# Rope angles traced one step later, and the row swaps of q and k issued by SyncE a step after their products

## The chip, the cores and the metric

The kernel runs on one core of a Trainium2 chip. The metric is the device time of one execution in microseconds (us). PE is TensorE, ACT ScalarE, DVE VectorE, POOL GpSimd, and SP SyncE, which only issues DMAs here.

## The reference

Two decoder layers on a (1, 1024, 1024) float32 stream. Each layer projects the stream with one wide matrix, runs three token mixers on the result, merges them with gates, projects back and normalises; then a gated MLP with a short convolution. The change touches the partial rotary embedding of q and k in the attention mixer, the first quarter (16) of each head's 64 channels:

```python
def rope_tables(positions):
    inv_freq = ROPE_THETA ** (-jnp.arange(0, ROT_DIM, 2, dtype=jnp.float32) / ROT_DIM)
    ang = positions.astype(jnp.float32)[..., None] * inv_freq
    return jnp.cos(ang), jnp.sin(ang)

def apply_partial_rope(t, cos, sin):
    half = ROT_DIM // 2
    x1, x2, rest = tf[..., :half], tf[..., half:ROT_DIM], tf[..., ROT_DIM:]
    out = jnp.concatenate([x1 * c - x2 * s, x2 * c + x1 * s, rest], axis=-1)
...
    proj = jnp.einsum('bsd,de->bse', x, w_in)
    u_pool, q, k, v, xc, gate_b, gate_c, gate_logits = jnp.split(proj, ...)
    q = apply_partial_rope(q.reshape(B, S, N_Q_HEADS, HEAD_DIM), cos, sin)
    k = apply_partial_rope(k.reshape(B, S, N_KV_HEADS, HEAD_DIM), cos, sin)
```

## The kernel before

Channels lie on the 128 partitions and the 1024 positions along the free axis. Every float32 operand is split into a high part (`scalar.copy` to fp32r, line 90) and a remainder (a subtraction, line 94, on DVE or POOL), and each product is three matmuls (lines 110 to 112).

The input projection of a layer works through 20 **pairs** of 128-column weight tiles, by a Strassen-like scheme of seven block products. One block product (`run`) is four blocks of three matmuls, 12 matmuls of 128x512. A pair has two halves. `begin` loads the first weight tile (`load(0)`, 512 KB, line 707, issued by SP), splits its two blocks and makes two runs (B11, B21); ACT copies the first sum out of PSUM (line 727). `rest` loads the second weight tile (`load(1)`, also line 707), forms block sums on POOL (line 741, then line 738 three times: a21, a11, and last a12), splits the results (`made`), and makes five runs in the order T2, T1, T3, T4, B22. The first of these, T2, needs the operand `w2`, which is `made(a11)`: it exists only after `load(1)` has landed, POOL has run lines 741, 738 and 738, and ACT has cast it. T2 also overwrites the PSUM bank that line 727 copies. Lines 759, 762 and 764 (DVE) put the pair's two outputs `ca` and `cb` together; 764 comes last and completes `ca`. Then `then(ca, cb)` hands them on.

`run_pairs` sets the order: begin, rest, begin, rest; the first two and the last two pairs are interleaved differently. After each half `due()` advances a tick and calls what `after(ticks, f)` has set aside, so `after(2, f)` called inside the `rest` of one pair runs f after the `begin` of the next pair and before its `rest`. Counting from 0, pair 2 makes k and v, pairs 4 and 6 make two 128-channel chunks of q each, and the pairs between make gates. The same holds in both layers.

For k and for each chunk of q, `turn` calls `swapped`: ACT copies the chunk (line 340), then four DMAs of 8 rows (32 KB each, lines 342 and 343) overwrite 32 rows of the copy with the partner rows. `rotate` (DVE, lines 349 to 351) follows by `after(3)`, and the split and the stores to DRAM by `after(4)`.

The cosine and sine tables: `rope_tables` (lines 156 to 178) fetches the positions by eight small POOL DMAs, works out angles on DVE (lines 163 to 170) and ACT (171 to 174), and ACT writes rows to DRAM. `rope_spread` (lines 182 to 193) has SP copy these rows over the partitions. At the start of layer 0, `second()` (lines 230 to 252) forms the blocks T2, T1, T3, T4 and B22 of the input on DVE and ACT.

The program is traced under

```python
with self.tc.manual_schedule(engines={mybir.EngineType.SP, mybir.EngineType.PE}):
```

SP and PE therefore issue in the order of the program text. The order on ACT, DVE and POOL is chosen by a planner when the program is built: from what it estimates to be ready, with the earlier place in the program as the priority.

Buffers that matter here: three weight tiles (`ws`), six split operands (`w`), three tiles `pt` (swap copies, and the sine table).

Of the kernel before, what the change touches and what calls it, by code (L numbers as in the profile page):

```python
# [60 lines left out]
class Trunk:  # L61
# [274 lines left out]
    def swapped(self, c):  # L336

        nc = self.nc
        swp = self.new([P, S], F32, "pt")
        nc.scalar.copy(swp[:], c[:])  # L340
        for base in (0, 64):
            nc.scalar.dma_start(swp[base:base + 8, :], c[base + 8:base + 16, :])
            nc.scalar.dma_start(swp[base + 8:base + 16, :], c[base:base + 8, :])
        return swp

    def rotate(self, c, swp, cos, sin):
# [28 lines left out]
    def project(self, l, first):  # L375

        nc = self.nc
        st = {}

        def turn(c, put):  # L380
            swp = self.swapped(c)
            self.after(3, lambda: self.rotate(c, swp, *self.tab))
            self.after(4, lambda: put(*self.parts(swp, c)))

        def kv(k, v):
            if l:
                self.load_tables()

            def put(hi, lo):
                for n in range(2):  # L390
                    own, other = slice(64 * n, 64 * n + 64), slice(64 - 64 * n, P - 64 * n)
                    self.store(self.kd[n, own], hi[own])
                    self.store(self.kd[n, other], lo[own])

            def keys_first():
                for c in range(2):
                    pt = self.bank()
                    for i in range(4):
                        b = 4 * c + i
                        nc.tensor.transpose(pt[:, i * P:(i + 1) * P], v[:, b * P:(b + 1) * P], self.ident[:])  # L400
                    t = self.new([P, 2, HALF], F32, "pt")
                    t = t[:].bitcast(F32R)
                    self.split(t[:, 0], t[:, 1], pt[:])
                    self.store(self.vd[:, :, c * HALF:(c + 1) * HALF].rearrange("a p c -> p a c"), t)

            turn(k, put)
            self.after(2, keys_first)

        def qq(i):
            def then(*c):  # L410
                for j in range(2):
                    def put(*x, j=j):
                        for n in range(2):
                            self.store(self.qd[:, :, n, 2 * i + j, :].rearrange("b c q -> c b q"),
                                       x[n].rearrange("c (b q) -> c b q", q=P))
                    turn(c[j], put)
            return then
# [48 lines left out]
        made, second = first or (None, None)  # L466
        if second:
            self.pend.append(lambda: None)
            self.pend.append(lambda: (second(), self.rope_tables()))
            self.after(4, self.parameters)  # L470
            self.after(2, self.rope_spread)
        self.run_pairs([self.pair([self.ins["w_in"][l, 2 * n + i] for i in range(2)], True, then,
# [628 lines left out]
```

## Time and profile before

| | |
|---|---|
| time, three runs | 2769.86, 2775.11, 2777.68 us; median 2775.11 |
| profiled execution, own time | 2775.4 us |
| its span | 2773.4 us |
| mean granted PE clock | 0.971 |
| busy: PE, DVE, POOL, ACT | 93%, 69%, 53%, 44% of the span |
| SP and ACT DMA issues | SP issues all weight loads; ACT the gates and 40 row swaps |

The profiled execution is one run taken by the hardware profiler; its span is the time from its first to its last instruction, and 2.0 us of its own time lie around that. In a timeline each row has the start and the duration in us, the engine (a trailing q: the engine's sequencer, as for a DMA issue), the line, the operation, the tiles (out<-in), how many instructions were merged (x), and in brackets the idle time before it and what ended that. PE busy is not PE at its peak, because matmuls are pipelined.

### The profile page before, as it was taken

How to read it: one execution, taken by the hardware profiler on the slowest of the kernel's cores; microseconds unless marked ns; L12 is line 12 of the kernel's file. 1: busy time of each engine (PE TensorE's matmuls, PEld its weight loads, DVE VectorE, ACT ScalarE, POOL GpSimd, SP SyncE). 2: the span in 40 equal slices, each digit the busy share in tenths (PEclk: the TensorE clock that was granted, in tenths of full speed). 3: DMA queues.
4: the chain of work that ended last, by engine and by line, in shares of the span. 5: the costliest groups of instructions: out<-in, count | busy, mean ns of one | idle time of the engine just before them, and what ended most of it. 6: DMA issues, size and time to landing. Idle time of an engine off the chain costs nothing.

```text
span 2773.4 us, 32010 instructions
## 1 busy us (share of the span) xinstructions
PE 2583.8 (93%) x11408; PEld 2105.9 (76%) x11408; DVE 1919.5 (69%) x2310; ACT 1233.4 (44%) x2050; POOL 1457.2 (53%) x962
## 2 busy tenths in 40 slices
PE   5989999998899999899889999999988999998887
PEld 4868887787688888677667788777867888877676
DVE  6565556737887877786675656477478887767866
ACT  4434445523544554434444444454335455544343
POOL 2554456767466555370434545566674556553701
PEclk8999999999999999999899999999999999999999
DMA  3433358554133333674323423765532333327742
GB/s 123 138 114 107 108 196 225 161 181 150 57 104 114 114 99 107 222 277 134 106 95 117 142 75 108 237 189 164 201 122 75 96 107 103 114 92 266 267 139 76
DMA packets 163232, 389.59 MB, mean 140 GB/s; under 512 B 17408, under 2 KB 48896, under 8 KB 162048
## 3 DMA queue, kind: packets, MB, share of 16 engines
q1 hardware_dynamic: 136496, 293.02, 32.3%
q0 software_dynamic: 14848, 55.09, 7.0%
q10 hardware_dynamic: 11728, 39.45, 3.7%
q8 instruction: 89, 1.46, 0.2%
q14 instruction: 71, 0.58, 0.1%
HBM read 281.75 MB, written 104.43 MB: 139 GB/s over the span
## 4 chain that ended last, share of the span: by engine, by line
PE 49%; DVE 16%; issue 5%; DMA 3%; ACT 3%; POOL 3%; ACTq 0%; DVEq 0%; SPq 0%; POOLq 0%
PE b L111 16%; PE b L112 16%; PE b L110 16%; DVE w L94 3%; DVE X L94 2%; DVE st L259 1%; DVE ve L275 1%; DMA X<-in_w_down 1%; POOL ws L738 1%; DVE pt L811 1%; ACT w L90 1%; POOL w L94 1%; DVE t L290 1%; DMA X<-h_blocks 1%; DVE w L321 0%
## 5 line engine op out<-in xcount | busy, mean ns | idle before, releaser
L110 PE MATMUL b<-X,w 128*128 128x512 f32 x2552 | 1014.1, 397 | 55.1 <-ACT s L727 20.0
L112 PE MATMUL b<-X,w 128*128 128x512 f32 x2552 | 1008.3, 395 | 27.9 <-DVE w L94 18.6
L111 PE MATMUL b<-X,w 128*128 128x512 f32 x2552 | 1006.5, 394 | 3.2 <-DVE X L94 3.2
L94 DVE TENSOR_TENSOR w<-ws,w 128x512 fp32r<-128x512 f32 (+1 forms) x454 | 450.4, 996 | 358.5 <-ACT w L90 346.3
L90 ACT CAST w<-ws 128x512 fp32r<-128x512 f32 (+1 forms) x608 | 408.0, 677 | 489.6 <-PE b L112 154.5
L110 PEld LDWEIGHTS b<-X,w 128*128 128x128 f32 x2552 | 487.4, 191 | 167.5 <-ACT s L727 24.6
L112 PEld LDWEIGHTS b<-X,w 128*128 128x128 f32 x2552 | 486.9, 191 | 136.4 <-DVE w L94 22.5
L94 POOL TENSOR_TENSOR w<-ws,w 128x512 fp32r<-128x512 f32 (+2 forms) x154 | 297.5, 1934 | 532.5 <-ACT w L90 520.3
L111 PEld LDWEIGHTS b<-X,w 128*128 128x128 f32 x2552 | 487.3, 191 | 105.9 <-DVE X L94 5.5
L741 POOL TENSOR_TENSOR ql<-ws 128x512 f32<-128x512 f32 x82 | 125.0, 1524 | 354.8 <-DMA ws<-in_w_in 254.0
L111 PE MATMUL b<-w,w 128*128 128x512 f32 x528 | 214.4, 406 | 48.5 <-DVE w L94 41.3
L110 PE MATMUL b<-w 128*128 128x512 f32 x528 | 211.1, 400 | 2.7 <-DVE pt L905 1.4
L112 PE MATMUL b<-w,w 128*128 128x512 f32 x528 | 210.6, 399 | 0.0
L111 PEld LDWEIGHTS b<-w,w 128*128 128x128 f32 x528 | 102.0, 193 | 82.4 <-DVE w L94 54.3
L738 POOL TENSOR_TENSOR ws<-ws,ws 128x512 f32<-128x512 f32 x82 | 142.4, 1736 | 6.2
L811 DVE SCALAR_TENSOR_TENSOR q<-t,par,q 128x1023 f32<-128x1023 f32 x88 | 127.4, 1448 | 19.0 <-ACT q L808 18.1
L94 DVE TENSOR_TENSOR w<-X,w 128x512 fp32r<-128x512 f32 (+1 forms) x107 | 121.5, 1158 | 22.3 <-ACT w L90 22.3
L738 POOL TENSOR_TENSOR ws<-ql,ws 128x512 f32<-128x512 f32 x82 | 125.0, 1524 | 6.3
L738 POOL TENSOR_TENSOR ws<-ws 128x512 f32<-128x512 f32 x82 | 118.6, 1446 | 16.9 <-DVE w L94 12.7
L110 PEld LDWEIGHTS b<-w 128*128 128x128 f32 x528 | 102.0, 193 | 28.3 <-DVE t L905 2.7
L811 DVE SCALAR_TENSOR_TENSOR pt<-t,par,pt 128x1023 f32<-128x1023 f32 x88 | 123.3, 1401 | 0.2
L112 PEld LDWEIGHTS b<-w,w 128*128 128x128 f32 x528 | 102.1, 193 | 20.6
(242 smaller groups left out, 3783.6 us busy)
## 6 DMA issues: line engine op xcount, KB each, us to landing
ws<-in_w_up SPq DMA_DIRECT2D x88, 512.0 KB
ws<-in_w_in SPq DMA_DIRECT2D x75, 512.0 KB
gates<-t ACTq DMA_DIRECT2D x48, 512.0 KB
ws<-in_w_o SPq DMA_DIRECT2D x40, 512.0 KB
h_blocks<-t SPq DMA_DIRECT2D x80, 256.0 KB
s<-h_blocks SPq DMA_DIRECT2D x66, 256.0 KB
t<-gates SPq DMA_DIRECT2D x32, 512.0 KB
t<-q_parts POOLq DMA_DIRECT2D x64, 256.0 KB, 4.1
```

The lines of the kernel that those rows point to most:

```text
L90: self.nc.scalar.copy(hi, src)
L94: return eng.tensor_tensor(lo, src, hi.bitcast(F32), op=ALU.subtract)
L110: self.nc.tensor.matmul(out, wh, xh, start=start and i == 0, stop=False, skip_group_check=more)
L111: self.nc.tensor.matmul(out, wh, xl, start=False, stop=False, skip_group_check=more)
L112: self.nc.tensor.matmul(out, wl, xh, start=False, stop=stop and i == n - 1, skip_group_check=more)
L259: self.nc.vector.bn_stats(st[:, c, :], z[:, c * HALF:(c + 1) * HALF])
L275: nc.vector.scalar_tensor_tensor(ve[:], ve[:], r[:], r[:], op0=ALU.mult, op1=ALU.mult)
L290: nc.vector.scalar_tensor_tensor(z[:], z[:], mv[:, 0:1], g[:], op0=ALU.subtract, op1=ALU.mult)
L738: sub = lambda out, x, y: nc.gpsimd.tensor_tensor(out, x, y, op=ALU.subtract)
L741: nc.gpsimd.tensor_tensor(s1[:], a21, a22, op=ALU.add)
L811: nc.vector.scalar_tensor_tensor(y[:, d:], c[:, :S - d], w(k), y[:, d:], op0=ALU.mult, op1=ALU.add)
```

## The change

Three edits. `swapped` issues its four DMAs on SP (`nc.sync`) and no longer on ACT. `turn` calls `swapped` two ticks later: after the `begin` of the next pair, ahead of its `rest`; `rotate` and the split stay at ticks 3 and 4. `rope_tables` is called one tick on, after the `rest` of the first pair, and not right behind `second()`.

```diff
@@ swapped
         for base in (0, 64):
-            nc.scalar.dma_start(swp[base:base + 8, :], c[base + 8:base + 16, :])
-            nc.scalar.dma_start(swp[base + 8:base + 16, :], c[base:base + 8, :])
+            nc.sync.dma_start(swp[base:base + 8, :], c[base + 8:base + 16, :])
+            nc.sync.dma_start(swp[base + 8:base + 16, :], c[base:base + 8, :])
@@ project
         def turn(c, put):
-            swp = self.swapped(c)
-            self.after(3, lambda: self.rotate(c, swp, *self.tab))
-            self.after(4, lambda: put(*self.parts(swp, c)))
+            swp = []
+            self.after(2, lambda: swp.append(self.swapped(c)))
+            self.after(3, lambda: self.rotate(c, swp[0], *self.tab))
+            self.after(4, lambda: put(*self.parts(swp[0], c)))
...
         if second:
             self.pend.append(lambda: None)
-            self.pend.append(lambda: (second(), self.rope_tables()))
+            self.pend.append(second)
+            self.after(1, self.rope_tables)
             self.after(4, self.parameters)
             self.after(2, self.rope_spread)
```

## The prediction

> **What bounds the kernel now.** I read the page first, then the waits of PE in the two input projections, then the timelines of the engines around each swap.
>
> ```profile
> span 2773.4 us, 32010 instructions
> PE 2583.8 (93%) x11408; PEld 2105.9 (76%) x11408; DVE 1919.5 (69%) x2310; ACT 1233.4 (44%) x2050; POOL 1457.2 (53%) x962
> ```
>
> PE sets the pace, so any time that PE stands still in a projection goes onto the end. Its waits, first for 0 to 400 us (layer 0), then for 1400 to 1850 us (layer 1), as total, times, longest:
>
> ```profile
> PE b L110 <- ACT w L90: 15.2, 1, 15.2
> PE b L110 <- ACT s L727: 9.1, 5, 4.4
> ...
> PE b L110 <- ACT s L727: 8.9, 4, 4.8
> ```
>
> One wait of 15.2 us at the start (it ends at 36.8), and a few for the copy of line 727. The four long ones of those stand in PE's timeline, each behind a pair that made q (pairs 4 and 6, layers 0 and 1):
>
> ```profile
> 147.56 0.50 PE L110 MATMUL b<-X,w 128*128 128x512 f32 x1 [4.37 <-ACT s L727]
> ...
> 192.75 0.79 PE L110 MATMUL b<-X,w 128*128 128x512 f32 x1 [2.86 <-ACT s L727]
> ...
> 1523.70 0.80 PE L110 MATMUL b<-X,w 128*128 128x512 f32 x1 [4.76 <-ACT s L727]
> ...
> 1567.98 0.79 PE L110 MATMUL b<-X,w 128*128 128x512 f32 x1 [2.50 <-ACT s L727]
> ```
>
> These matmuls open run T2 of the pair that follows (5 or 7). ACT's timeline says why the copy is late. At 147.56 us:
>
> ```profile
> 140.46 2.00 ACT L340 COPY pt<-t 128x1024 f32<-128x1024 f32 x2 [0.92 <-DVE t L764]
> 141.55 0.65 ACTq L342 DMA_DIRECT2D pt<-t  x1
> ...
> 146.25 0.63 ACTq L343 DMA_DIRECT2D pt<-t  x1
> 146.92 0.59 ACT L727 COPY s<-b 128x512 f32<-128x512 f32 x1 [4.46 <-DMA pt<-t]
> ```
>
> The two copies start when DVE line 764 has completed the chunk. Then ACT issues eight swap DMAs, (146.25 - 141.55) / 7 = 0.67 us apart, and only then copies the sum that T2 waits for. Removing this is worth at most the four waits, 4.37 + 2.86 + 4.76 + 2.50 = 14.5 us, and the slow matmuls after them (below).
>
> **Part 1: the swaps on SP.** ACT loses 40 issues (four for each of five chunks in two layers), and line 727 can follow the copies at once. SP gets the 40, and SP's order is that of the program: `load(0)` of the next pair, then the swaps, then `load(1)` of the next pair, then `load(0)` of the one after. What matters is when those loads are issued now, and when a swap can be. SP in the stretch before the first stall:
>
> ```profile
> 121.85 0.33 SPq L707 DMA_DIRECT2D ws<-in_w_in  x1
> ...
> 141.10 0.33 SPq L707 DMA_DIRECT2D ws<-in_w_in  x1
> ```
>
> Counting loads from the start, the one at 121.85 is `load(1)` of pair 5 and the one at 141.10 `load(1)` of pair 6. So pair 5's is out 25.7 us ahead of its T2 (147.56). After the change it stands behind eight swaps of pair 4's chunks, which cannot go before the copy that ends at 141.5. That SP keeps its order and that a waiting issue holds those behind it is seen where `rope_spread` waited for a memset:
>
> ```profile
> 54.71 0.91 DVE L183 MEMSET q<- 128x1024 f32 x1 [0.16 <-DVE w L94]
> ...
> 55.69 0.35 SPq L188 DMA_DIRECT2D q<-rope_rows  x1
> ...
> 57.05 0.29 SPq L188 DMA_DIRECT2D q<-rope_rows  x1
> 57.38 0.29 SPq L189 DMA_DIRECT2D pt<-rope_rows  x1
> ...
> 59.35 8.19 SPq L707 DMA_DIRECT2D ws<-in_w_in  x2
> ```
>
> The first spread goes as the memset ends at 55.62, and the next weight load only behind all eight, at 59.35.
>
> Behind the held `load(1)` lies this chain, shown by pair 5 (130.11 to 135.40) and pair 6 (from 145.41):
>
> ```profile
> 130.11 1.28 POOL L741 TENSOR_TENSOR ql<-ws 128x512 f32<-128x512 f32 x1 [10.22 <-DMA ws<-in_w_in]
> ...
> 134.07 1.29 POOL L738 TENSOR_TENSOR ws<-ql,ws 128x512 f32<-128x512 f32 x1
> 145.41 1.26 POOL L741 TENSOR_TENSOR ql<-ws 128x512 f32<-128x512 f32 x1 [8.66 <-DMA ws<-in_w_in]
> ...
> 151.19 2.16 POOL L738 TENSOR_TENSOR ws<-ql,ws 128x512 f32<-128x512 f32 x1
> 135.40 0.62 ACT L90 CAST w<-ws 128x512 fp32r<-128x512 f32 x1 [5.17 <-POOL ws L738]
> ```
>
> - Issue to landing: 141.10 to 145.41, 4.3 us.
> - POOL to a11: three operations, 1.28 + 2 x 1.29 and gaps = 4.0 us undisturbed; 1.26 + 2 x 2.16 and gaps = 5.7 us beside the rotations on DVE, which will run at this time. I take 5.5. With other work put between, as now for pair 6, it is 151.19 + 2.16 - 145.41 = 7.9.
> - ACT's cast: 0.65 with its start.
>
> So T2 can start 4.3 + 5.5 + 0.65 = 10.45 us after the last swap issue. Eight swaps at ACT's 0.67 us are 5.35 us. No row shows a swap issued by SP; the nearest SP rows, the spreads of eight rows from DRAM above, go (59.35 - 55.69) / 8 = 0.46 us apart at most, and 0.33 between neighbours. I take 0.67, because ACT's rows are the same transfer, SBUF to SBUF, and keep 0.33 as the low end. The sum runs from the first issue of each swap, which the copy sets and which need not move:
>
> ```profile
> 100.15 1.23 ACTq L342 DMA_DIRECT2D pt<-t  x1
> ...
> 186.40 0.65 ACTq L342 DMA_DIRECT2D pt<-t  x1
> ...
> 1476.37 0.66 ACTq L342 DMA_DIRECT2D pt<-t  x1
> ...
> 1517.36 0.65 ACTq L342 DMA_DIRECT2D pt<-t  x1
> ...
> 1561.96 0.65 ACTq L342 DMA_DIRECT2D pt<-t  x1
> ```
>
> For q, T2 starts 15.8 us after the first issue: 157.35, 202.2, 1533.15 and 1577.75, later than now by 9.8, 9.4, 9.5 and 9.8, together 38.5 us. Those differences already include that the waits for line 727 go. For k there is one chunk, four swaps, 2.7 + 10.45 = 13.15 us: 113.3 and 1489.5. T2 of pair 3 starts now, without a stall, right behind eight transposes:
>
> ```profile
> 104.38 0.48 PE L110 MATMUL b<-X,w 128*128 128x512 f32 x1
> ...
> 1480.60 0.48 PE L110 MATMUL b<-X,w 128*128 128x512 f32 x1
> ```
>
> That is 8.9 us later in each layer, 17.8 us, two stalls that are not there now.
>
> A stall also costs afterwards. PE's granted clock behind the first one, by two stretches of 3.7 us (PE busy and matmuls come first, the clock stands ahead of the DMA share):
>
> ```profile
> 147.50:151.20 3.70, 3.64 (x9) 2.81 (x10) 3.67 (x3) 1.05 (x3) 3.62 (x3) 0.57 0.06 9
> 151.20:154.90 3.70, 3.70 (x17) 3.09 (x16) 3.70 (x4) 2.05 (x3) 3.70 (x2) 0.97 0.02 1
> ```
>
> 9 matmuls where 17 fit: 3.7 x 8 / 17 = 1.7 us lost. The four q stalls pay that already; the two for k are new, 3.4 us. The Trainium skill, "TensorE: Matmul & The Clock Gate", Part 1, says that PE falls to half rate after an idle window of about 3.4 us. By it the gaps of 2.86 and 2.50 us would mostly be spared now and their longer successors not: 3.4 us more on the sum. The rows of 192.75 and 1567.98 (first matmul 0.79 us) show both already paying, so I leave that out.
>
> The Trainium skill, "DMA: Bandwidth & Descriptors", Anatomy of one DMA, fits 2.0 us + bytes / 436 GB/s for a DMA issued by GpSimd: an estimate of 3.2 us for 512 KB against the 4.3 us here. By it the six loads would take 6.6 us off the sum; the measured one stands.
>
> Sum of part 1: 38.5 + 17.8 + 3.4 = 59.7 us. Low end: issues 0.33 us apart, the last four of q also waiting for the second copy (ending 142.46), save 3.0 us four times and 1.35 twice; undisturbed POOL saves 1.5 six times; 59.7 - 14.7 - 9.0 = 36. High end: POOL at 7.9 us adds 2.4 six times, 74.
>
> What hides the rest: the rotations still start when swaps land, a time that does not move, and nothing needs k and q before the merge; zero. The later load also delays `load(0)` of the pair after, but that has PE's whole `rest`, five runs of 12 matmuls at 0.22 us (13 us), and only then is it wanted; zero. A `pt` tile is taken at the same copy; zero.
>
> **Part 2: the angles.** They lie in the 15.2 us wait at the start:
>
> ```profile
> 18.89 1.28 POOL L741 TENSOR_TENSOR ql<-ws 128x512 f32<-128x512 f32 x1 [2.66 <-DMA ws<-in_w_in]
> 19.05 1.18 DVE L163 CAST angles<-angles 128x64 f32<-128x64 int32 x1 [2.25 <-DMA angles<-in_positions]
> ...
> 25.87 0.20 DVE L170 TENSOR_SCALAR angles<-angles 128x64 f32<-128x64 f32 x1
> ...
> 30.76 1.22 DVE L240 TENSOR_TENSOR w<-t,pt 128x1024 f32<-128x1024 f32 x1
> ```
>
> DVE spends 19.05 to 26.07 on angles, and the blocks of x (line 240 on) start at 30.76. But line 163 is already the later one in the program text: it is called after line 240 there and runs ahead of it on DVE. The planner put it there because it believed nothing earlier in the text was ready. The change moves it behind the `rest` of pair 0 as well, whose work needs a weight tile that SP loads after the tiles of line 240 (it lands at 18.89). If line 240 was not ready in the plan, neither was that. So I expect the same order and cost this at zero. Bounds: if the angles do leave, line 240 could start as soon as DVE falls idle at 19.05 - 2.25 = 16.8, a gain of 30.76 - 16.8 = 14 us at most, less the 7 us of DVE that come back in a stretch where PE waits for DVE. Loss: none that I find, since the spread rows are wanted at 55.69 and only eight DMA rows follow.
>
> **The rivals.**
> 1. *The load is not held, and only the gain remains* (the other side). Then the four waits and their slow matmuls go, 14.5 + 4 x 1.7 = 21 us: 2775.4 - 21 = 2754. It holds if `load(1)` is out by 147.56 - 10.45 = 137.1. For it: weights are fetched 25 us ahead. Against: the swap's copy starts at 140.46, after that point, and SP keeps its order. Chance 0.05; in it 0.01 for a gain eaten up to no change.
> 2. *The stalls come, and the angles leave the start.* 59.7 - 7 = 53: 2828. For it: 7 us of DVE in PE's longest wait. Against: the order shown. Chance 0.15.
> 3. *POOL takes the split of the rotated chunk before a11.* Now it follows a11 (which ends at 153.35):
>
> ```profile
> 153.36 2.80 POOL L94 TENSOR_TENSOR t<-t,pt 128x1024 fp32r<-128x1024 f32 x1
> 156.10 0.93 POOL L691 DMA_DIRECT2D q_parts<-pt  x1
> ```
>
> But the chunk will be rotated about when the held load lands. The split and its two DMA issues would add 2.8 + 2 x 0.9 = 4.6 us in each of four places, 18 us: 2853. Chance 0.15.
> 4. My forecast, all of part 1 and nothing of part 2: 2775.4 + 59.7 = 2835. Chance 0.65.
>
> **How the numbers follow.** The profiled execution's own time is 2775.4, 0.3 above the median, so I forecast 2835. The range goes from 2801 (low end 36, less 10 for part of the angles) to 2854 (rival 3). The measurement tells about 0.3%, 8 us, from no change; faster 0.04, same 0.01, slower 0.95.
>
> **What would show it.** In the changed trace: the swaps as SP rows just before a `load(1)`; PE waits of 9 to 15 us at T2 of pairs 3, 5 and 7 in both layers, ended by ACT's cast of w2 (line 90) and behind that POOL waiting for its weight DMA; line 727 no longer behind swap DMAs; at the start, line 163 still before line 240. I am wrong if the `load(1)` of pair 5 stands before the swaps, if a swap issue on SP takes 0.3 us, or if the 15.2 us wait at the start shrinks.

## The result, and the profile after

The changed kernel takes 2864.06 us (median of 2861.64 to 2868.07) against 2777.68 us for the kernel before on the same chip: a ratio of 1.0319 on record, interval 1.0303 to 1.0335 (the two medians alone give 1.0311). I had forecast 2835 and no more than 2854. The direction and the hold of the weight load came as forecast; the medians differ by 86.4 us where the sum had 59.7, so about 27 us were missing from it. One run of `late_on_act` below took 5616.04 us, twice its other four, without a trace and for a reason that stays open; the median given there is that of the four.

In the changed kernel the lines of the later functions stand two further down (707 is now 709, 727 is 729, 738 and 741 are 740 and 743, 764 is 766); 340 to 351 keep their numbers. The page's head, then TensorE's waits from 60 to 420 us and from 1400 to 1850 us (total, times, longest):

```profile
span 2860.5 us, 32037 instructions
PE 2601.4 (91%) x11408; PEld 2118.5 (74%) x11408; DVE 1916.8 (67%) x2310; ACT 1235.4 (43%) x2050; POOL 1449.5 (51%) x962
```

```profile
PE b L110 <- ACT w L90: 39.2, 3, 15.9
PE b L110 <- ACT s L729: 5.7, 2, 3.1
...
PE b L110 <- ACT w L90: 38.5, 3, 15.4
PE b L110 <- ACT s L729: 5.0, 2, 2.7
```

The work is the same: TensorE's busy time grows by 17.6 us, at a mean granted clock of 0.956 against 0.971, and the other engines' busy times change by less than 8 us. The rest of the new time is waiting. In each layer TensorE waits three times for ACT's cast of `w2` (line 90), at T2 of pairs 3, 5 and 7. SyncE's queue and ACT at the first q chunks show the forecast hold:

```profile
151.36 0.65 SPq L342 DMA_DIRECT2D pt<-t  x1
...
156.44 0.62 SPq L343 DMA_DIRECT2D pt<-t  x1
157.17 0.85 SPq L709 DMA_DIRECT2D ws<-in_w_in  x2
```

```profile
150.28 2.00 ACT L340 COPY pt<-t 128x1024 f32<-128x1024 f32 x2 [4.78 <-DVE t L766]
152.28 0.59 ACT L729 COPY s<-b 128x512 f32<-128x512 f32 x1
159.67 1.04 ACT L90 CAST pt<-t 128x1024 fp32r<-128x1024 f32 x1 [6.80 <-DVE t L351]
...
169.88 0.62 ACT L90 CAST w<-ws 128x512 fp32r<-128x512 f32 x1 [3.62 <-POOL ws L740]
```

Eight swaps, (157.17 - 151.36) / 8 = 0.73 us apart, stand ahead of the weight load. Line 729 now follows the copies at once, as foretold. But the cast comes 169.88 - 157.17 = 12.7 us after the load's issue, where I had 4.3 + 5.5 = 9.8. POOL's timeline and TensorE's say what lies between, and what comes a pair later:

```profile
160.79 3.31 POOL L94 TENSOR_TENSOR t<-t,pt 128x1024 fp32r<-128x1024 f32 x1 [22.84 <-DMA ws<-in_w_in]
164.05 0.93 POOL L693 DMA_DIRECT2D q_parts<-pt  x1
...
165.89 1.27 POOL L743 TENSOR_TENSOR ql<-ws 128x512 f32<-128x512 f32 x1
...
171.15 2.82 POOL L94 TENSOR_TENSOR t<-t,pt 128x1024 fp32r<-128x1024 f32 x1
...
175.72 1.64 POOL L94 TENSOR_TENSOR w<-ws,w 128x512 fp32r<-128x512 f32 x1
```

```profile
170.55 0.80 PE L110 MATMUL b<-X,w 128*128 128x512 f32 x1 [15.58 <-ACT w L90]
...
194.90 0.80 PE L110 MATMUL b<-X,w 128*128 128x512 f32 x1 [3.12 <-ACT s L729]
```

The split of the first rotated chunk (160.79) and its two stores run ahead of line 743. That is rival 3, and the order is the same at the other three q stalls (splits at 221.95, 1583.54 and 1644.17). The split of the second chunk (171.15), with its stores, stands ahead of POOL's remainder at 175.72. Beside both, DVE forms pair 5's remainders, and slowly: the three that follow the one of `w2` take 2.85, 1.78 and 1.77 us, where `split_on_dve` below has 0.68 for each. The last of these three is shown here from DVE's timeline, then SyncE's longest wait for a weight tile between 150 and 200 us, and the load that follows it:

```profile
176.14 1.77 DVE L94 TENSOR_TENSOR w<-ws,w 128x512 fp32r<-128x512 f32 x1
...
SPq L709 <- DVE w L94: 17.1, 1, 17.1
...
177.99 0.88 SPq L709 DMA_DIRECT2D ws<-in_w_in  x2
```

That remainder ends at 177.91, and the load leaves 0.08 us later. It is `load(1)` of pair 6, which before was out at 141.10; with three weight tiles it takes the one of `load(0)` of pair 5, whose last reader in the kernel's text is the remainder of a12, on DVE. Pair 6's T2 then waits 3.12 us at 194.90 (before 0.83, at 170.55): a wait that I had costed at nothing. What comes last there is not `w2` but line 729. Three rows of ACT, then one of DVE, show why:

```profile
186.96 0.62 ACT L90 CAST w<-ws 128x512 fp32r<-128x512 f32 x1 [8.16 <-POOL ws L740]
...
192.81 1.05 ACT L460 ACTIVATE t<-t 128x1024 f32<-128x1024 f32 x1
...
194.26 0.59 ACT L729 COPY s<-b 128x512 f32<-128x512 f32 x1 [0.40 <-ACT t L460]
...
187.61 1.24 DVE L94 TENSOR_TENSOR w<-ws,w 128x512 fp32r<-128x512 f32 x1 [8.50 <-ACT w L90]
```

ACT stood 8.16 us at the cast of pair 6's `w2`, and DVE 8.50 us at its remainder, because the load was late. Pair 5's sums on DVE (lines 761 to 766), its two gates on ACT (line 460) and, behind these, line 729 came only after that.

At the start of the kernel nothing changed: line 163 still runs before line 240, and TensorE's first long wait ends at 36.62 (before 36.8). Its length reads 13.69 us against 15.2 because the matmuls ahead of it end later, not because it ends earlier.

```profile
19.01 1.21 DVE L163 CAST angles<-angles 128x64 f32<-128x64 int32 x1 [2.23 <-DMA angles<-in_positions]
...
30.60 1.22 DVE L240 TENSOR_TENSOR w<-t,pt 128x1024 f32<-128x1024 f32 x1
36.62 0.79 PE L110 MATMUL b<-X,w 128*128 128x512 f32 x1 [13.69 <-ACT w L90]
```

To put the lost time in its places, I take the DVE row that completes a pair (line 766, before 764) in both traces; for pair 4:

```profile
139.75 0.68 DVE L764 TENSOR_TENSOR t<-s,b 128x512 f32<-128x512 f32 x1
...
149.56 0.69 DVE L766 TENSOR_TENSOR t<-s,b 128x512 f32<-128x512 f32 x1 [1.96 <-PE b L112]
```

Pair 4 is 149.56 - 139.75 = 9.8 us late. The table does the same at the rows of pairs 4, 6 and 8, in both layers. Each figure is what the one profiled execution lost on the way to that row, in us; "between" is from pair 8 of layer 0 to pair 0 of layer 1. The row of `angles_alone`, whose time did not change, tells how far to trust a figure: it reads up to 1.5 us where nothing was lost. For the same swaps, the changed kernel and `swaps_alone` differ by 2.9 us in "between".

| kernel | layer 0: k, first q, second q | between | layer 1: k, first q, second q |
|---|---|---|---|
| forecast | 10.6, 9.8, 9.4 | 0 | 10.6, 9.5, 9.8 |
| changed kernel | 9.8, 15.9, 16.3 | 4.6 | 10.2, 16.0, 16.0 |
| `angles_alone` | 0.4, -0.3, 0.4 | 1.5 | -0.1, -0.2, 0.4 |
| `swaps_alone` | 9.1, 15.5, 16.7 | 7.5 | 10.3, 16.3, 16.0 |
| `split_on_dve` | 8.5, 10.2, 12.1 | 10.5 | 10.3, 11.0, 10.5 |
| `pool_free` | 9.7, 10.2, 10.6 | 6.1 | 10.1, 10.6, 10.2 |
| `pool_free_half` | 8.9, 9.9, 9.6 | 6.7 | 8.6, 9.1, 10.1 |
| `k_alone` | 10.1, 0.0, 0.6 | 1.9 | 10.4, 0.6, 0.3 |
| `late_on_act` | -0.4, 3.0, 6.2 | 8.9 | 0.0, 2.6, 5.6 |
| `swaps_behind_rest` | 5.5, -1.3, -0.6 | 6.7 | 6.5, -0.9, -1.0 |
| `pair_later` | -0.8, -3.4, -4.9 | 6.2 | 0.1, -3.1, -5.0 |
| `pair_later2` | 2.2, -4.2, -4.4 | 1.6 | 2.5, -4.0, -4.5 |
| `pair_later_free` | 0.1, -6.5, -4.9 | 6.3 | 0.6, -5.2, -5.4 |

### The profile page after: what moved, and what is told of

Its sections match the earlier page's. It is cut to its first block, busy times and chain, and to the rows that moved or that the text cites. A ratio compares the mean times of both kernels' runs of the same rounds, so it can differ in the third digit from the quotient of the medians.

```text
span 2860.5 us, 32037 instructions
## 1 busy us (share of the span) xinstructions
PE 2601.4 (91%) x11408; PEld 2118.5 (74%) x11408; DVE 1916.8 (67%) x2310; ACT 1235.4 (43%) x2050; POOL 1449.5 (51%) x962
## 5 line engine op out<-in xcount | busy, mean ns | idle before, releaser
L112 PEld LDWEIGHTS b<-w,w 128*128 128x128 f32 x528 | 102.3, 194 | 20.7
```

Source lines behind the costliest of these rows:

```text
L112: self.nc.tensor.matmul(out, wl, xh, start=False, stop=stop and i == n - 1, skip_group_check=more)
```

## The experiments

**The parts alone.** `angles_alone` keeps the third edit only, `swaps_alone` the first two.

> Only the angles are traced one tick later; the swaps stay on ACT and where they were. Theory (planner keeps the order): line 163 runs on DVE at about 19 us as before, PE's first long wait ends at 36.6 to 36.8 us, and the time is that of the kernel before, 2777 within 4 us. Rival (the angles leave the start and something later pays for it, so that the changed kernel hides a gain): PE's wait at the start is 8 to 13 us shorter and the time is 2765 to 2770.

> Part 1 of the change alone: the swaps on SyncE at the second callback, the angles as before. The angles alone gave no difference, so if the parts do not act on one another 2864, between 2860 and 2868; if the later angles make room or trouble for the swaps, another time by more than 4 us.

Angles alone: 2775.29 us, ratio 0.9993 (0.9984 to 1.0002). Swaps alone: 2860.67 us (2857.95 to 2870.76), ratio 1.0305 (1.0286 to 1.0324), which takes in the changed kernel's 1.0319. So part 2 does nothing that these runs can tell from zero, and part 1 is the whole loss.

**Is it SyncE's order, the place or POOL?** Three variants of the changed kernel. `late_on_act` issues the swaps on ACT again, at the later tick:

```diff
-            nc.sync.dma_start(swp[base:base + 8, :], ...)   # all four
+            nc.scalar.dma_start(swp[base:base + 8, :], ...)
```

> The changed kernel with the swaps issued by ACT again, at the changed place in the program (two ticks late). Theory (SP's queue holds load(1)): nothing is held, no wait of PE for the cast of w2, ACT delays line 729 as in the kernel before, 2770 to 2785. Rival (the later place itself costs, because the rotation and the split come later and meet the next pair's work): 2820 or more.

`swaps_behind_rest` calls them one tick later, behind `load(1)`:

```diff
-            self.after(2, lambda: swp.append(self.swapped(c)))
+            self.after(3, lambda: swp.append(self.swapped(c)))
```

> The changed kernel with one number altered: the swaps on SP one tick later still, behind the rest of the next pair (after 3 instead of 2), so that load(1) of the next pair stands ahead of them on SP. Theory (the held load(1) is what costs): load(1) of pair 5 is issued at about 122 us again, the waits of 8 us for k and 15 us for q go, the waits for line 727 of the kernel before go too, and the time is 2754 to 2768, under the kernel before. Rival (a swap on SP costs by itself, by its transfer or by what DVE and POOL do later): 2800 or more.

`pool_free` takes the rotated chunks' work off POOL:

```diff
-            self.after(4, lambda: put(*self.parts(swp[0], c)))
+            self.after(4, lambda: put(*self.parts(swp[0], c, "vector")))   # remainder on DVE
...
-                            self.store(self.qd[...], x[n]...)               # POOL
+                            nc.scalar.dma_start(self.qd[...], x[n]...)
```

> The changed kernel, but the remainders of the rotated k and q are formed by DVE and q's parts are stored by DMAs that ACT issues, so that POOL has nothing between load(1) landing and the block sums. Theory A (POOL takes the split and two stores of a rotated chunk ahead of line 743, 4.5 us in each of four places): the four waits of 15.5 us fall to about 11 and the time to 2840 to 2850. Theory B (the four waits are long because the load itself lands late): no shorter than 15, 2860 to 2870.

- `late_on_act`: 2797.93 us, ratio 1.0069 (1.0055 to 1.0083), outside both expected ranges. With SyncE's hold gone 66.1 us come back, but not all. TensorE waits 10.2 and 6.5 us for the copies of lines 729 and 755 in layer 0. Line 755 runs behind ACT's late swap issues (to 150.34, the copy at 150.91); line 729 behind the two gates, as in the changed kernel.

```profile
PE b L110 <- ACT s L729: 10.2, 3, 6.0
PE b L110 <- ACT s L755: 6.5, 2, 3.2
```

- `swaps_behind_rest`: 2785.03 us, ratio 1.0032 (1.0022 to 1.0043), a miss against the 2754 to 2768 of the theory. The waits of 15 us are gone, but the load behind pair 4's swaps is then `load(0)` of pair 6, and TensorE waits for DVE's remainders (line 94) instead, five times in layer 0; the way from that load to these waits was not followed up:

```profile
PE b L112 <- DVE w L94: 8.8, 5, 2.6
```

- `pool_free`: 2841.07 us, ratio 1.0226 (1.0212 to 1.024). The 23 us that it gains on the changed kernel are what POOL's work on the rotated chunks cost. That is within theory A's range, though the long waits of layer 0 fall from 15.6 and 15.9 us only to 13.1 and 13.4, not to 11. In its trace line 743 starts as the load lands, 160.56 - 156.87 = 3.7 us after the issue, with nothing ahead:

```profile
156.87 16.96 SPq L709 DMA_DIRECT2D ws<-in_w_in  x4
...
160.56 2.24 POOL L743 TENSOR_TENSOR ql<-ws 128x512 f32<-128x512 f32 x1 [22.76 <-DMA ws<-in_w_in]
```

**Split or stores?** `split_on_dve` has the remainders on DVE and leaves the stores on POOL.

> The changed kernel with the remainders of the rotated chunks on VectorE and q's two stores left on GpSimd: it tells apart what the split (3.31 us) and the stores (0.93 and 0.90 us) each add to a stall of q. Theory A (both stand in front of the first add of the load in need, line 743): the stores, issued when VectorE has the remainder, end some 2 us after the load has landed, 4 x 2 = 8 us on the 2841 us of the run without both: 2849, between 2846 and 2854. Theory B (the split alone costs, the stores find a gap): 2841 within 3.

Measured: 2846.0 us, ratio 1.0244 (1.023 to 1.0258). That is the lower edge of theory A's range, but the 5 us to `pool_free` are not shown to be the stores: the intervals of the two ratios overlap, and the spans of the two profiled executions are 0.5 us apart (2842.2 and 2842.7). The stores do run ahead of line 743, which starts at 161.82 where the load is due at 155.81 + 3.7 = 159.5; yet in the two projections this kernel loses only 62.6 us against 61.4 of `pool_free` (sums of the table). So of the two, the split is the cost in the projections: (15.9 + 16.3 + 16.0 + 16.0) - (10.2 + 12.1 + 11.0 + 10.5) = 20.4 us at the four q places. What the split does a pair later shows too. DVE's three remainders behind the one of `w2` take 0.68 us each here; the third ends at 171.21, and `load(1)` of pair 6 follows at 171.29, against 177.99 in the changed kernel. Of these 6.7 us, 2.3 are there when T2 starts (168.21 against 170.55), and 4.4 are the slow remainders:

```profile
170.53 0.68 DVE L94 TENSOR_TENSOR w<-ws,w 128x512 fp32r<-128x512 f32 x1
```

```profile
171.29 1.98 SPq L709 DMA_DIRECT2D ws<-in_w_in  x2
```

TensorE's waits for line 729 (5.7 and 5.0 us in the two projections of the changed kernel) are gone in this kernel and in `pool_free`.

**Is the rest the hold, and its length the issue time?** `k_alone` is the kernel before with only k's swap on SyncE at tick 2. `pool_free_half` is `pool_free` with `for base in (0,)`.

> The kernel before, with only k's four swap transfers moved to SyncE half a pair later; q's swaps and the angles stay as they were. Theory A (SyncE holds the load behind the swaps; at k the GpSimd engine is not occupied by the split): 11 us in each of the two layers, so the 2777.7 us of before + 2 x 10.6 = 2799, between 2793 and 2805. Theory B (what the other places lose, 14.5 us each, is lost at every swap alike, the split of the rotated chunk aside): 2 x 14.5 = 29, about 2807. Theory C (the start of the swaps half a pair later is itself what costs, as with the swaps late on ScalarE): some 20 us whatever issues them, of which k has a third: 2785.

> The changed kernel with the remainders of the split on VectorE and q's stores on ScalarE (2841 us), and with only the first two of the four swap transfers; the rows from 64 on are then not swapped, so that part of the rotation is left out. Theory A (the issue of the transfers lies on the path, 0.68 us each): four holds of q shorter by 2 x 0.68 = 1.36 us, two holds of k by as much, and every stall at half rate the longer or shorter with it: 6 x 1.36 = 8 us at full, 13 us with the half rate, so 2828 to 2833. Theory B (the load waits for the cast, not for the transfers' issue, and these only lie behind it): no change, 2841 within 3.

`k_alone`: 2798.04 us, ratio 1.0078 (1.0066 to 1.0091), 20.7 us more than its kernel before; theory A had 21. TensorE's one wait for the cast in a layer:

```profile
PE b L110 <- ACT w L90: 7.7, 1, 7.7
```

`pool_free_half`: 2834.5 us, ratio 1.0207 (1.0192 to 1.0223). That lies between the two expected ranges, 6.6 us under `pool_free`, and the two intervals overlap, so the timing alone decides little. The expectation also counted two issues fewer per q where there are four, 2.7 us; 13.5 us in all would have been right. The waits for the cast do shrink by about that much per q, from 13.4 to 10.5 us at the longest, and in layer 0 from 34.2 to 28.3 us together (k's own does not: 7.7 and 8.4). But the wait for DVE's remainder behind it grows from 2.7 to 6.3 us and takes back 3.6 of those 5.9:

```profile
PE b L110 <- ACT w L90: 34.2, 3, 13.4
PE b L112 <- DVE w L94: 2.7, 3, 0.9
```

```profile
PE b L110 <- ACT w L90: 28.3, 3, 10.5
PE b L112 <- DVE w L94: 6.3, 2, 4.3
```

The first fence is `pool_free`, the second `pool_free_half`, both 60 to 420 us. So the issue time lies on the way to the cast of q; with half of it gone, DVE's remainder is next.

**A place where the load has time.** `pair_later` moves the whole chain on by a pair, `pair_later2` the same with the rotation in the swaps' tick and the halves one later, `pair_later_free` is `pair_later` with `pool_free`'s edits.

```diff
-            self.after(2, lambda: swp.append(self.swapped(c)))
-            self.after(3, lambda: self.rotate(c, swp[0], *self.tab))
-            self.after(4, lambda: put(*self.parts(swp[0], c)))
+            self.after(4, lambda: swp.append(self.swapped(c)))
+            self.after(5, lambda: self.rotate(c, swp[0], *self.tab))
+            self.after(6, lambda: put(*self.parts(swp[0], c)))
```

> The changed kernel with the swaps on SyncE one half-pair pair of steps later still (at the fourth callback instead of the second, the rotation at the fifth, the halves at the sixth), so that SyncE has the three loads of the next pairs out before it comes to the swaps, and the load behind them waits for its buffer in any case. Theory A (only the hold of the load in need costs): the 15 us waits of TensorE are gone and line 729's wait too, 2754 to 2770. Theory B (each later place takes time from the merges, as with the swaps late on ScalarE, 2800, and behind the rest, 2785): 2785 to 2800.

> As the run with the swaps two callbacks later, but with the rotation asked for in the same callback as the swaps and the halves one later: the swapped copy is held shorter. Theory A: 2754 to 2770, as there. Theory B: 2785 to 2800, as there; if the held copy is what takes the time of the merges, this run stands between the two, 5 us or more under the other.

> The run with the swaps two callbacks later (2761 us), with the remainders on VectorE and q's stores on ScalarE as well. Theory A (GpSimd's work costs only while a load in need stands behind it, and q's parts come late into attention there, a wait of 4.9 us in layer 0): stores earlier by some 2 us, 2 to 10 us faster: 2751 to 2759. Rival (the VectorE and ScalarE work lies on the way of the evictions now that TensorE does not wait): same or slower, 2761 to 2768.

`pair_later`: 2760.97 us, ratio 0.9946 (0.9934 to 0.9959). `pair_later2`: 2766.9 us, ratio 0.9963 (0.995 to 0.9976). `pair_later_free`: 2756.52 us, ratio 0.9925 (0.9913 to 0.9937). All three lie in theory A's ranges and beat both kernels, if by less than 1%. `pair_later2` is not faster than `pair_later`, so nothing shows that the held copy costs. SyncE's queue in `pair_later`: two weight loads go out ahead of the swaps, and the first one behind them is `load(1)` of pair 6, issued 5.2 us later than the 141.10 of before.

```profile
127.55 3.10 SPq L709 DMA_DIRECT2D ws<-in_w_in  x2
140.76 0.65 SPq L342 DMA_DIRECT2D pt<-t  x1
...
145.62 0.62 SPq L343 DMA_DIRECT2D pt<-t  x1
146.35 0.85 SPq L709 DMA_DIRECT2D ws<-in_w_in  x2
```

TensorE's waits in layer 0 (60 to 420 us) are then small, and the longest stands in attention, for the stored q:

```profile
PE b L500 <- DMA t<-q_parts: 4.9, 1, 4.9
PE b L110 <- ACT s L729: 1.7, 2, 1.4
```

So the hold of a load in need, and what it displaces, is what costs, not SyncE as the issuer nor the later place as such. `pair_later_free` shortens the wait for q only to 4.2 us; its further 4.5 us, with intervals that just overlap, come mainly from the pairs (the table's first q, -6.5 and -5.2).

## Why the prediction was wrong

- **Right: the angles.** I costed part 2 at zero from the order on DVE; the run alone gives 0.9993.
- **Right: the hold.** `load(1)` stands behind the swaps, and line 729's share is gone. With POOL's work on q taken away, k costs 9.7 and 10.1 us against 10.6 forecast, and q 10.2, 10.6, 10.6 and 10.2 against 9.8, 9.4, 9.5 and 9.8: together 61.4 us against 59.7. That it comes so close is in part luck, as the terms err both ways: swaps 0.73 us apart instead of 0.67, a landing of 3.7 us instead of 4.3, POOL's three operations 6.7 us (160.56 to 167.24) instead of 5.5. For the landing, the Trainium skill, "DMA: Bandwidth & Descriptors", Anatomy of one DMA, with its fit for a DMA issued by GpSimd, gave an estimate of 3.2 us; the row lies about midway.
- **Wrong: the weighing of rival 3.** I took a11 ahead of the split, as in the trace before, and gave the other order 0.15. The new trace has the split first at the q stalls, and so rival 3, at 2853, was the likelier case. Rows of before would have made it at least even:

```profile
146.23 1.52 DVE L349 TENSOR_TENSOR t<-t,q 128x1024 f32<-128x1024 f32 x1 [5.20 <-DMA pt<-t]
...
157.16 1.21 DVE L350 TENSOR_TENSOR pt<-pt,pt 128x1024 f32<-128x1024 f32 x1
```

  Line 349 began 4.7 us after the first swap issue (141.55), three undisturbed rotation steps take some 3 x 1.22 = 3.7 us, and the cast 1.05: the split is ready 9.4 us after the first issue. The load needs 8 x 0.67 + 4.3 = 9.7 us from the same moment. In the changed kernel:

```profile
156.01 1.23 DVE L349 TENSOR_TENSOR t<-t,q 128x1024 f32<-128x1024 f32 x1 [0.25 <-DMA pt<-t]
...
158.41 1.23 DVE L351 TENSOR_TENSOR t<-t,pt 128x1024 f32<-128x1024 f32 x1
```

  With the cast up to 160.71 that is 9.4 us from 151.36, while the load, with 3.7 us from 157.17, is due at 160.9. POOL's order is the planner's, and its own estimates are in no trace, so this shows only that the order was open, not why the planner chose so.
- **Wrong: the size and place of that cost.** Rival 3 said 4.6 us directly ahead of a11. The first split adds less: from load to cast there are 12.7 us in the changed kernel, 167.54 - 155.81 = 11.7 in `split_on_dve`, 167.24 - 156.87 = 10.4 in `pool_free`: POOL's first three operations take some 1.27 us each in the changed kernel and 2.1 to 2.2 in `pool_free`, beside DVE's rotations, so part of what the split costs is won back. Most comes a pair later, by the step where I wrote "zero" for what hides the rest. I had looked at `load(0)` of the next pair only. The second split, and the POOL remainder behind it, slow DVE's remainders, the last of these holds the weight tile, and so `load(1)` of the next pair; that holds ACT and DVE, and so line 729: the 3.12 us at 194.90, and matmuls at half rate after it. Together 20.4 us at four places instead of 18.
- **Probably wrong: nothing between the layers.** I had written that nothing needs k and q before the merge, but attention does. The changed kernel loses 4.6 us there; of the other kernels that start q's chain later, eight lose 6.1 to 10.5 us, but `pair_later2` only 1.6, about as little as `angles_alone`. With one profile of each, the size of this term is not settled. At the start of attention TensorE waits 3.5 us for the stored q in the changed kernel and 4.9 in `pair_later`, against 2.6 before. The first line is before's, the second the changed kernel's:

```profile
PE b L498 <- DMA t<-q_parts: 2.6, 2, 1.9
```

```profile
PE b L500 <- DMA t<-q_parts: 3.5, 1, 3.5
```

  That accounts for about 1 us in the changed kernel. What the rest is stays open.

The sum, from unrounded figures: 61.4 (the hold, from `pool_free`) + 20.4 (the split) + 2.5 (stores and k, the rest of the 84.3 in the two projections) + 4.6 (between) - 1.9 (behind them, not followed up) = 87.0 us, the difference of the two spans, 2860.5 and 2773.4; the medians differ by 86.4. So the step that failed is that the split of the rotated chunks costs nothing: its place ahead of a11 was taken for the unlikely case, and the wait that it causes a pair later was put at zero. That is 20.4 of the missing 27 us; the rest lies between the layers and in terms of 1 to 3 us.

The wait of 3.12 us is followed by slow matmuls, 0.80 and then 0.63 us instead of 0.39, at a granted clock of 0.50 from 194.8 to 196.8 us:

```profile
195.50 0.63 PE L111 MATMUL b<-X,w 128*128 128x512 f32 x1
```

The Trainium skill, "TensorE: Matmul & The Clock Gate", Part 1, has half rate after an idle window of about 3.4 us; here a shorter wait is enough, as the two rows of before in the prediction said; after the 2.55 us at 255.63 the third matmul takes 0.63 us too.

## What to carry to other kernels

When DMAs are put on the queue that fetches weights, list for each load behind them how long it can wait, and place them where the next one has time: a pair later, the same move gained 0.5% instead of losing 3%. A held load shifts the order on the engines that a planner arranges, so work out for each of them when every competing step is ready; if two times lie within a few tenths of a microsecond, take the bad order as likely. Then ask which buffer that work holds or which other engine it slows, and which load waits for the buffer.

## What was not expected of the hardware

A subtraction on DVE can take four times as long beside one on POOL. In the changed kernel the remainder of `ql` runs beside POOL's second split (171.15 to 173.97); in `split_on_dve` it does not:

```profile
171.67 2.85 DVE L94 TENSOR_TENSOR w<-ql,w 128x512 fp32r<-128x512 f32 x1
```

```profile
169.33 0.68 DVE L94 TENSOR_TENSOR w<-ql,w 128x512 fp32r<-128x512 f32 x1
```

The Trainium skill, "GPSIMD Engine Reference", Specifications, lists the SBUF interfaces as shared with VectorE, in contention with DVE instructions that have two SBUF inputs. Both rows are such instructions, and the trace agrees: 2.85 us against 0.68.

The changed kernel's trace shows more of it. The slow row ends 0.55 us after POOL's split does (174.52 and 173.97), and so does the one that frees the weight tile (177.91 and 177.36). Of the 648 remainders of this size on DVE, 273 begin while a POOL operation on two tensors runs, and 267 of these end 0.54 to 0.60 us after that operation; the 338 that meet none take 0.64 to 0.69 us. In these rows DVE's subtraction in effect waits for POOL's operation to end.
